# The mLSTM's second half moved up beside the last RWKV units, and the token-shift tile in buffers of its own

## The chip, the cores and the metric

The kernel runs on one core of a Trainium2 chip. The metric is the device time of one launch in microseconds; lower is better. TensorE runs at one of two clock levels, 1.2 and 2.4 GHz; the profile gives the granted clock as a share of the higher one.

## The reference, cut to what matters

A model of one mixing block with two kinds of recurrence, and two attention layers, on 1024 tokens of width 1024, in float32:

```python
z = rmsnorm(x, norm1) @ w_in              # 26 units of 128 columns, and 8 gate columns
y_r = rwkv7_group(z[:, :RW_COLS], ...)    # token shift, then 8 heads of 64: S <- S*decay + ..., y = S r
y_m = mlstm_group(z[:, RW_COLS:], ...)    # conv on q and k, then 4 heads of the chunkwise mLSTM, gated by o
x = x + concat([y_r, y_m]) @ w_out
x = x + ffn(rmsnorm(x, norm2))            # 22 pairs of gate and value columns, with a causal conv
for l in range(2): x = x + attention_layer(x, l)
```

The mLSTM divides its output by a normalizer, takes an RMS norm over each head, and multiplies by a gate:

```python
h = num / jnp.maximum(jnp.abs(den), jnp.exp(-m_t))[..., None]
y = head_rmsnorm(h) * mh_norm_g * sigmoid(o)
```

## The kernel before

Every float32 product of the projections is made from a high and a low part: `mm3` issues three matmuls of 128x128 by 128x512, weight-high by input-high, weight-high by input-low, weight-low by input-high. One such matmul is called a product here; they are numbered from 0 in the order of the program, and there are 11,328. Weights are loaded (`wraw`) by SP's DMA queue and split by ScalarE (`whi`) and VectorE or GpSimd (`wlo`), in `wsplit`. A helper `few` does the eight gate columns in 32 smaller matmuls on weights of its own (`few_split`).

The input projection runs in units of 128 columns, each in two halves of 512 tokens. 14 units belong to RWKV (`RW`), 12 to the mLSTM (`ML`). `unit` evicts a half: an RWKV unit is scaled into a tile `rq`, shifted by a token and mixed (`stage`) and stored to `pT` in memory. `rq`, with one buffer, is also the tile of the convolution and of the `few` weights. The scale `BC` of a half comes from `first_scale`: an rsqrt by VectorE (`nry`), transposes on TensorE (`p<-c_ident,nry`, the broadcast), and a copy.

Beside the products run two recurrences in small matmuls. RWKV works in 8 units of 128 tokens (units 0 to 7). For a unit it prepares operands, inverts a triangular matrix for eight heads (`Z`, `X`, their diagonals `ZD`, `XD`, `Y`, `GD`), refines it (`AA`, `GT`, `TT`), runs two chunks (`RH`, `UV`, state `S`, output `P`), and then normalizes and gates the output (`out`: `YS`, `yva`, `yry`, transposes into PSUM tile `e`, `YQ`, and `sg,wug`, the gate, into `e` again). The mLSTM works in 8 blocks of 128 tokens (`ml_block`): transposes of `rv`, keys, scores `SD`, the state `C`, the numerator `NUM`, denominator `den`, `HN` with its norm (`mr...`), transposes of `HN`, and the store of the result to `yd`. Blocks 0 to 3 are the first half, 4 to 7 the second.

PSUM banks come from pools: `e` (pool `pse`) has one bank. The operands of RWKV stand on the right side of the memory in pools `rc`, `re`, `ro` and others; `re`, with one buffer, holds the first operands of a unit. `ml1` is the mLSTM's second half; `rest` first closes RWKV's whole room (`right.close()`) and then opens pools `mx` and `my` and two banks for it. Behind it comes, for each half of the tokens (`half1`), the out projection, which loads the results (`xo<-yd`) and splits them (`act<-xo`), and the FFN. The out projection of the first half runs early; that of the second begins at product 2448, and needs the whole second half of the mLSTM.

A scheduler sets the order of each engine; an engine runs its instructions in that order. `pace(groups, start, n)` gives it a rule: product `start + i*n` may not be issued ahead of group i (a group is a run of small matmuls without another engine's work between them):

```python
for groups, start, n in self.paces:
    for i, g in enumerate(groups):
        j = int(start + i * n)
        if g is not None and j < len(self.gm):
            self.tc.add_manual_dep(self.gm[j].ins, g.ins.name, dep, reason="order")
```

So a pace is a deadline of the group, not its earliest time. `g2` is product 960. RWKV's groups are paced from `g2 + NB0`, 1160, four products apart; the 40 groups of `ml1` (ten to a block) from `g2 + NC0`, 2002, twelve apart, so that the last comes before product 2470.

Of the kernel before, what the change touches and what calls it, by code (L numbers as in the profile page):

```python
# [25 lines left out]
NEG = -1.0e30  # L26
NW1 = 26
NW2 = 52
NA0, NA, NM0, NM, NB0, NB, NC0, NCC, SP0, SP1 = 60, 4, 30, 12, 200, 4, 1042, 12, 7, 11
NS0 = 60  # L30
NG = 6
PA = 56, 1, 48, 1
# [96 lines left out]
class Kern:  # L129
# [170 lines left out]
    def block1(self, yd):  # L300
        nc, ap, tc = self.nc, self.ap, self.tc
        gR, gK, gV, gL = (self.dram([128, n, T], "pT") for n in (4, 4, 4, 2))
        gQ, gW, gO = (self.dram([128, 4, T], "pT") for _ in range(3))
# [3 lines left out]
                 + [(gO, j) for j in range(4)])  # L307
        RW = [12, 13] + list(range(12))
        ML = list(range(14, 26))
        right = ExitStack()  # L310
        with self.pools(stg=2, bcp=1, a1=2, psl=1) as (stg, bcp, a1, psl):
            BC = self.t(bcp, [128, 2, 512], "BC")
            acts = [None, self.new_act(a1)]
# [8 lines left out]
            def unit(j, halves, w=None, ps=None):  # L322
                w = w or self.wsplit(ap["w_in"][j])
                g, i = where[j]
                for hf in halves:
                    acc = self.gemm(w, acts[hf], ps=ps)
                    if j < 14:

                        rq = self.t(stg, [128, 515], "rq", bufs=1)[:, 0:513]
                        if hf == 0:  # L330
                            nc.vector.memset(rq[:, 0:1], 0.0)
                        else:
                            nc.vector.tensor_copy(rq[:, 0:1], shalo[:, j:j + 1])
                        self.tt(rq[:, 1:513], acc, BC[:, hf])
                        st = self.t(stg, [128, 512], "stage")
                        self.act(st, rq[:, 1:513], scale=omu[:, j:j + 1])
                        self.stt(st, rq[:, 0:512], self.par("mu", j), st)
                        if hf == 0:
                            nc.vector.tensor_copy(shalo[:, j:j + 1], rq[:, 512:513])
                        nc.sync.dma_start(g[:, i, hf * 512:hf * 512 + 512], st)  # L340
                        continue
                    st = self.t(stg, [128, 512], "stage")
                    if g is gQ:

                        rq = self.t(stg, [128, 515], "rq", bufs=1)
                        if hf == 0:
                            nc.vector.memset(rq[:, 0:3], 0.0)
                        else:
                            nc.vector.tensor_copy(rq[:, 0:3], halo[:, i])
                        self.tt(rq[:, 3:515], acc, BC[:, hf])  # L350
                        if hf == 0:
                            nc.vector.tensor_copy(halo[:, i], rq[:, 512:515])
                        cv = self.t(stg, [128, 512], "cv", bufs=1)
                        self.act(cv, rq[:, 0:512], AF.Identity, bias=cwh[:, 16 + i:17 + i], scale=cwh[:, i:i + 1])
                        for n in range(1, 4):
                            self.stt(cv, rq[:, n:n + 512], cwh[:, 4 * n + i:4 * n + i + 1], cv)
                        self.act(st, cv, AF.Tanh)
                        self.stt(st, st, 1.0, cv, op0=ALU.add, op1=ALU.mult)
                    else:
                        self.tt(st, acc, BC[:, hf])  # L360
                    nc.sync.dma_start(g[:, i, hf * 512:hf * 512 + 512], st)

            with self.pools(a0=2) as a0:
                acts[0] = self.new_act(a0)
                with self.pools(x0=4, nrm=2) as (xp, sp):
                    with self.pools(psw=4) as psw:
                        w = [self.wsplit(ap["w_in"][j]) for j in RW[:2]]
                        st = self.first_load(xp, sp, 0, acts[0])
                        self.first_scale(sp, psl, st, BC, 0)
                        for i in range(2):  # L370
                            unit(RW[i], (0,), w[i], psw)
                        st = self.first_load(xp, sp, 1, acts[1])
                        for j in RW[2:4]:
                            unit(j, (0,), None, psw)
                    self.first_scale(sp, psl, st, BC, 1)
                for j in RW[4:NG]:
                    unit(j, (0,))
                ws = self.few_split(stg, "cv", stg, ap["w_g"], 8, "rq")
                for hf in range(2):
                    sg = self.t(stg, [8, 512], "stage")  # L380
                    self.few(stg, ("stage", 2), ws, 8, acts[hf], sg)
                    self.tt(sg, sg, BC[0:8, hf])
                    nc.sync.dma_start(gG[:, hf * 512:hf * 512 + 512], sg)
                with self.pools(side="right", mr=1) as mr:
                    G = self.ml_gates(self.mk, mr, psl, gG)
                    for j in RW[NG:]:
                        unit(j, (0,))
                names = dict(rc=1, re=1, ro=1, r2=2, r3=3, rx=1, psm=2, psc=1, pse=1)
                R = dict(zip(names, right.enter_context(self.pools(side="right", **names))))
                rw = self.rwkv(R, gR, gK, gV, gL, yd[0])  # L390
                g0 = len(self.gm)
                ga = [x for _ in range(4) for x in next(rw)]
                for j in ML:
                    unit(j, (0,))
# [13 lines left out]
                self.pace(gb, g2 + NB0, NB)  # L408
                self.pace(ga, g0 + NA0, NA)

        def ml1(mx, my, ps):
            gm = self.ml_blocks(range(4, 8), self.mk, mx, my, ps, G, gQ, gW, gO, yd[1])
            self.pace(gm, g2 + NC0, NCC)

        if self.stop == "mix":
            right.close()
            with self.pools(mx=1, my=2, psl=1) as (mx, my, psl):
                ml1(mx, my, psl)
            self.mks.close()
            for i in range(2):  # L420
                for hf in range(2):
                    nc.sync.dma_start(
                        self.dbg["yT"].rearrange("(g k p) t -> p g k t", p=128, k=4)[:, i, :, hf * 512:(hf + 1) * 512],
                        yd[i][hf])
            return
        self.rest(yd, right, ml1)


    @contextmanager
# [57 lines left out]
        self.flush()  # L487
        return acc

    def rest(self, yd, right, ml1):  # L490
        self.psn = None
        ap = self.ap
        xd = [[self.dram([128, 512], "xd") for _ in range(2)] for _ in range(8)]
        F = [None, None]
        with self.pools(acA=2) as self.acA:
            with self.pools(**self.ffn_pools(0)) as P:
                right.close()
                with self.pools(side="right", mx=1, my=2, psl=2) as (mx, my, psl):
                    ml1(mx, my, psl)
                self.mks.close()  # L500
                F[0] = self.half1(0, P, self.acA, yd, xd)
                for _ in range(8):
                    next(F[0])
                rs = ExitStack()
                self.acB = rs.enter_context(self.pools(side="right", acB=2))
                with self.pools(side="right", psn=2) as self.psn, self.pools(side="right", **self.ffn_pools(1)) as P1:
                    F[1] = self.half1(1, P1, self.acB, yd, xd)
                    next(F[1])
                    for a0 in F[0]:
                        pass  # L510
                    for a1 in F[1]:
                        pass
# [624 lines left out]
        nc.vector.memset(C, 0.0)  # L1137
        return dict(bmd=bmd, TK=TK, DEC=DEC, trik=trik, C=C)

    def ml_blocks(self, blocks, mc, mx, my, psm, G, gQ, gW, gO, yd):  # L1140
        with self.collect() as g:
            for tb in blocks:
                self.ml_block(tb, mc, mx, my, psm, G, gQ, gW, gO, yd)
        return g

    def ml_block(self, tb, mc, mx, my, psm, G, gQ, gW, gO, yd):
        nc = self.nc
        bmd, TK, DEC, trik = (G[n] for n in ("bmd", "TK", "DEC", "trik"))
        C = G["C"]
# [6 lines left out]
        nc.sync.dma_start(rv, gW[:, :, ts_])  # L1156
        V1 = self.t(my, [128, 4, 130], "V1")
        nc.vector.memset(V1[:, :, 128:129], 1.0)
        pv = self.t(psm, [128, 4, 128], "p")
        for h in range(4):  # L1160
            self.tr(pv[:, h], rv[:, h], self.ident)
        self.act(V1[:, :, 0:128], pv)
# [7 lines left out]
        self.tt(DT, DT, trik[:, None, :].to_broadcast([128, 4, 128]), ALU.add, eng=nc.gpsimd)  # L1170
        for h in range(4):
            self.act(DT[:, h], DT[:, h], AF.Exp, bias=TK[:, tb, 0, h:h + 1])
        pk = self.t(psm, [128, 2, 128], "p")
        for j in range(2):
            self.tr(pk[:, j], QK[:, 2 + j], self.ident)
        KW = self.t(mx, [128, 4, 64], "KW")
# [2 lines left out]
        SD = self.t(mx, [128, 4, 128], "SD")  # L1179
        for i in range(2):  # L1180
            pr = slice(i * 64, i * 64 + 64)
            pst = self.t(psm, [128, 2, 128], "p")
            for h2 in range(2):
                self.mm(pst[:, h2], QK[pr, 2 + h2], QK[pr, h2])
            self.stt(SD[:, i:4:2], pst, 0.125, DT[:, i:4:2], op0=ALU.mult, op1=ALU.mult)
        NUM = self.t(mx, [128, 4, 130], "NUM")
        for i in range(2):
            pr = slice(i * 64, i * 64 + 64)
            pq = self.t(psm, [128, 2, 130], "p")
            for h2 in range(2):  # L1190
                self.mm(pq[:, h2, 0:129], QK[pr, h2], C[pr, h2, 0:129])
            for h2 in range(2):
                h = h2 * 2 + i
                self.act(NUM[:, h, 0:129], pq[:, h2, 0:129], scale=TK[:, tb, 3, h:h + 1])
        Cn = self.t(mc, [128, 2, 130], "C", bufs=2)
        pcs = self.t(psm, [128, 2, 130], "p")
        for h in range(4):
            h2, i = h // 2, h % 2
            self.mm(pcs[i * 64:i * 64 + 64, h2, 0:129], KW[:, h], V1[:, h, 0:129])
# [2 lines left out]
            pr = slice(i * 64, i * 64 + 64)  # L1202
            self.stt(Cn[pr, h2, 0:129], C[pr, h2, 0:129], DEC[pr, h, tb:tb + 1], pcs[pr, h2, 0:129])
        for h2 in range(2):
            pn = self.t(psm, [128, 2, 130], "p")
            for i in range(2):
                self.mm(pn[:, i, 0:129], SD[:, h2 * 2 + i], V1[:, h2 * 2 + i, 0:129])
            self.tt(NUM[:, 2 * h2:2 * h2 + 2, 0:129], NUM[:, 2 * h2:2 * h2 + 2, 0:129], pn[:, :, 0:129], ALU.add)
# [12 lines left out]
        self.ts(va, va, 1.0 / 128, 1e-6)  # L1221
        rs = self.rsqrt(mx, va, "mr")
        self.tt(HN, HN, rs[:, :, None].to_broadcast([128, 4, 128]))
        ph = self.t(psm, [128, 4, 128], "p")
        for h in range(4):
            self.tr(ph[:, h], HN[:, h], self.ident)
        YO = self.t(mx, [128, 4, 128], "SD")
# [489 lines left out]
```

## Time and profile before

| | |
|---|---|
| median of 3 runs | 3503.1 µs |
| runs | 3508.12, 3502.71, 3503.10 µs |
| the profiled execution's own time | 3496.53 µs |
| its span | 3494.7 µs |
| mean granted clock of TensorE | 0.984 |

The profile shows one execution on the chip. Times are microseconds from the start of the span. PE is TensorE's matmuls, PEld its weight loads, DVE VectorE, ACT ScalarE, POOL GpSimd, SPq the DMA queue of SyncE. A row of the timeline has start, duration, engine, line of the kernel, operation, written tile and read tiles, and the number of like instructions in a row; square brackets hold the idle time of the engine before it and what ended it. Almost every matmul has line 186 and every transpose line 189, since helpers issue them: they are told apart by their tiles. Matmul ends are modelled, so durations of matmuls in a row overlap.

### The profile page before, as it was taken

Reading aid. Unit: us, or ns where it says so; the run is one execution under the profiler, and the core shown is the slowest. Engines: PE = TensorE matmul, PEld = TensorE weight load, DVE = VectorE, ACT = ScalarE, POOL = GpSimd, SP = SyncE. Lnnn points to the kernel's source line nnn. Section 1 sums busy time; section 2 is a strip of 40 time slices with the busy share of each in tenths; the row PEclk is TensorE's granted clock in tenths of the full one; section 3 lists DMA queues with packets and bytes.
Section 4 is the critical chain, followed back from the end, with each engine's and each line's share of the span. In section 5 each row is a group of like instructions: output and inputs, shape, how many; then the busy total and the mean of one; then the engine's idle time right before and its main releaser. Section 6 shows DMA issues by size and latency. Waiting matters only on the chain.

```text
span 3494.7 us, 51106 instructions
## 1 busy us (share of the span) xinstructions
PE 3379.8 (97%) x18820; PEld 2730.9 (78%) x18820; DVE 2038.6 (58%) x4223; ACT 1609.1 (46%) x3244; POOL 702.6 (20%) x601
## 2 busy tenths in 40 slices
PE   7999999999899999999999999999999999999998
PEld 6777777777677777778888878888878888888886
DVE  6767767765655745467666762234776567712235
ACT  4467677654433433345555652122355456621222
POOL 1222122222122222242111111111321111111111
PEclk9999899999999999999999999999999999999999
DMA  4433233123333323333212121113531121211124
GB/s 149 155 115 103 79 112 102 56 68 111 102 113 94 128 91 91 94 121 89 55 55 66 45 88 58 43 53 110 158 98 55 48 67 51 79 53 60 50 71 142
DMA packets 196986, 303.51 MB, mean 87 GB/s; under 512 B 22976, under 2 KB 65600, under 8 KB 196736
## 3 DMA queue, kind: packets, MB, share of 16 engines
q1 hardware_dynamic: 196736, 300.25, 28.1%
q8 instruction: 148, 2.42, 0.3%
q14 instruction: 102, 0.84, 0.1%
HBM read 244.41 MB, written 38.98 MB: 81 GB/s over the span
## 4 chain that ended last, share of the span: by engine, by line
PE 51%; DVE 2%; ACT 2%; issue 1%; DMA 0%; SPq 0%; POOL 0%; DVEq 0%; ACTq 0%; POOLq 0%
PE p L186 31%; PE acc L186 10%; PE o L186 3%; PE t L189 3%; PE S L186 3%; ACT whi L166 0%; DMA qw<-qf 0%; DVE qf L172 0%; PE d L186 0%; DVE wlo L172 0%; SPq L1374 0%; DVE yt L172 0%; DVE dd L1458 0%; ACT act L166 0%; ACT dd L168 0%
## 5 line engine op out<-in xcount | busy, mean ns | idle before, releaser
L186 PE MATMUL p<-act,whi 128*128 128x512 f32 x5824 | 1893.4, 402 | 31.0 <-ACT act L166 22.1
L186 PEld LDWEIGHTS p<-act,whi 128*128 128x128 f32 x5824 | 1086.3, 190 | 265.5 <-ACT act L166 23.8
L186 PE MATMUL p<-act,wlo 128*128 128x512 f32 x2912 | 1162.4, 401 | 2.1 <-DVE wlo L172 2.0
L172 POOL TENSOR_TENSOR wlo<-wraw,whi 128x512 fp32r<-128x512 f32 (+1 forms) x366 | 501.8, 1371 | 1959.4 <-ACT whi L166 1738.7
L166 ACT ACTIVATE whi<-wraw 128x512 fp32r<-128x512 f32 x732 | 424.1, 620 | 777.2 <-PE p L186 324.0
L186 PEld LDWEIGHTS p<-act,wlo 128*128 128x128 f32 x2912 | 552.8, 190 | 123.0 <-DVE wlo L172 6.8
L172 DVE TENSOR_TENSOR wlo<-wraw,whi 128x512 fp32r<-128x512 f32 x366 | 286.4, 784 | 264.7 <-ACT whi L166 262.4
L168 ACT ACTIVATE dd<-dd,nm 128x256 f32<-128x256 f32 (+7 forms) x256 | 171.1, 669 | 107.5 <-DVE nm L1458 105.4
L166 ACT ACTIVATE th<-p 128x512 f32<-128x512 f32 x96 | 56.4, 588 | 307.5 <-PE p L186 287.1
L166 ACT ACTIVATE ph<-t 128x384 fp32r<-128x384 f32 (+1 forms) x248 | 135.4, 557 | 123.0 <-PE t L189 118.3
L172 DVE TENSOR_TENSOR pl<-t,ph 128x384 fp32r<-128x384 f32 (+1 forms) x248 | 156.2, 636 | 50.3 <-ACT ph L166 47.4
L183 DVE SCALAR_TENSOR_TENSOR th<-th,acc 128x512 f32<-128x512 f32 x64 | 43.9, 687 | 223.7 <-ACT th L166 223.5
L177 POOL TENSOR_SCALAR rx<-rd 128x128 f32<-128x128 f32 x128 | 72.1, 572 | 478.0 <-PE t L189 235.5
L189 PE MATMUL t<-c_ident,dd 128*128 128x128 f32 x900 | 152.8, 275 | 1.0 <-DVE yt L172 0.7
L172 DVE TENSOR_TENSOR xs<-xs,d 128x512 f32<-128x512 f32 x132 | 88.7, 684 | 98.8 <-PE d L186 97.5
L186 PE MATMUL o<-ph,V 128*128 128x256 f32 (+1 forms) x532 | 132.6, 282 | 1.7 <-ACT ph L166 1.6
L186 PE MATMUL o<-pl,V 128*128 128x256 f32 (+1 forms) x532 | 130.3, 291 | 0.1
L1458 DVE CUSTOM_DVE_ANT_0 dd<-S,strip 128x512 f32<-128x512 f32 (+3 forms) x160 | 91.5, 586 | 52.8 <-PE t L189 29.8
L189 PEld LDWEIGHTS t<-c_ident,dd 128*128 128x128 f32 x900 | 107.7, 141 | 11.1 <-DVE yt L172 1.5
L186 PE MATMUL d<-gl,whi 128*128 128x512 f32 x264 | 107.2, 406 | 6.3 <-DVE gl L172 6.3
L186 PE MATMUL d<-gh,whi 128*128 128x512 f32 x264 | 105.1, 411 | 7.0 <-DVE xs L172 5.2
L186 PEld LDWEIGHTS o<-ph,V 128*128 128x128 f32 x532 | 98.7, 190 | 14.7 <-ACT ph L166 4.3
(407 smaller groups left out, 5066.3 us busy)
## 6 DMA issues: line engine op xcount, KB each, us to landing
wraw<-in_w_in SPq DMA_DIRECT2D x332, 256.0 KB, 2.8
wraw<-in_w_up SPq DMA_DIRECT2D x176, 256.0 KB, 2.6
wraw<-in_w_out SPq DMA_DIRECT2D x96, 256.0 KB, 2.8
wraw<-in_w_dn SPq DMA_DIRECT2D x88, 256.0 KB, 2.7
pT<-stage SPq DMA_DIRECT2D x52, 256.0 KB, 3.8
qw<-qf SPq DMA_DIRECT2D x160, 64.0 KB, 2.0
xd<-xs SPq DMA_DIRECT2D x32, 256.0 KB, 3.0
yd<-yt SPq DMA_DIRECT2D x32, 256.0 KB, 2.3
```

The source lines that it names most:

```text
L166: return self.nc.scalar.activation(out, in_, func, scale=scale, **kw)
L168: return self.nc.scalar.activation(out, in_, func, bias=bias, scale=scale, **kw)
L172: (eng or self.nc.vector).tensor_tensor(out, a, b, op=op)
L177: (eng or self.nc.vector).tensor_scalar(out, a, s1, None, op0=op0)
L183: return self.nc.vector.scalar_tensor_tensor(out, a, s, b, op0=op0, op1=op1, **kw)
L186: return self.pe(self.nc.tensor.matmul(out, lhsT, rhs, start=start, stop=stop, **kw))
L189: return self.pe(self.nc.tensor.transpose(out, in_, ident))
L1458: nc.vector.tensor_tensor_reduce(dd[:, o:o + w], sps[:, :w], strip[:, o:o + w], -1.0, init, ALU.add, ALU.min, nm)
```

## The change

The shift of the RWKV units gets a tile `sh` with two buffers; `rq` stays with the convolution and the `few` weights. Pool `re` is opened in a stack of its own, `elems`. `ml1` closes that one alone, opens `mx` and `my` in its room, takes RWKV's bank `e` for its PSUM tiles instead of two banks of its own, and closes RWKV's remaining room behind it. It is paced from `g2 + 760`, product 1720, instead of 2002: the last group is due before product 2188.

```diff
-NA0, NA, NM0, NM, NB0, NB, NC0, NCC, SP0, SP1 = 60, 4, 30, 12, 200, 4, 1042, 12, 7, 11
+NA0, NA, NM0, NM, NB0, NB, NC0, NCC, SP0, SP1 = 60, 4, 30, 12, 200, 4, 760, 12, 7, 11
...
-        right = ExitStack()
+        right, elems = ExitStack(), ExitStack()
...
-                        rq = self.t(stg, [128, 515], "rq", bufs=1)[:, 0:513]
+                        rq = self.t(stg, [128, 513], "sh", bufs=2)
...
-                names = dict(rc=1, re=1, ro=1, r2=2, r3=3, rx=1, psm=2, psc=1, pse=1)
+                names = dict(rc=1, ro=1, r2=2, r3=3, rx=1, psm=2, psc=1, pse=1)
                 R = dict(zip(names, right.enter_context(self.pools(side="right", **names))))
+
+                R["re"] = elems.enter_context(self.pools(side="right", re=1))
...
-        def ml1(mx, my, ps):
-            gm = self.ml_blocks(range(4, 8), self.mk, mx, my, ps, G, gQ, gW, gO, yd[1])
+        def ml1():
+            elems.close()
+            with self.pools(side="right", mx=1, my=2) as (mx, my):
+                gm = self.ml_blocks(range(4, 8), self.mk, mx, my, R["pse"], G, gQ, gW, gO, yd[1], "e")
+            right.close()
             self.pace(gm, g2 + NC0, NCC)
...
-                right.close()
-                with self.pools(side="right", mx=1, my=2, psl=2) as (mx, my, psl):
-                    ml1(mx, my, psl)
+                ml1()
                 self.mks.close()
...
-    def ml_block(self, tb, mc, mx, my, psm, G, gQ, gW, gO, yd):
+    def ml_block(self, tb, mc, mx, my, psm, G, gQ, gW, gO, yd, tag):
...
-        pv = self.t(psm, [128, 4, 128], "p")
+        pv = self.t(psm, [128, 4, 128], tag)
```

Every PSUM tile of `ml_block` takes `tag` in this way.

The first place is TensorE at the sixth RWKV unit (`p_515`), the broadcast of the second half's scale (`p_454`), and the `few` products (`p_554` and `p_577`, 16 for each half of the tokens), as a piece of the difference of the two orders.

```order
 L186 MATMUL p_515<-act_115,whi_505 128x512
 L186 MATMUL p_515<-act_114,wlo_506 128x512
-L189 MATMUL p_454<-c_ident_60,nry_441 128x128 x4
 L186 MATMUL p_554<-act_114,rq_550 40x512
 L186 MATMUL p_554<-act_115,rq_550 40x512
```

```order
 L186 MATMUL p_577<-act_103,rq_550 40x512
 L186 MATMUL p_577<-act_104,rq_550 40x512
+L189 MATMUL p_454<-c_ident_60,nry_441 128x128 x4
 L186 MATMUL p_737<-act_114,whi_727 128x512
 L186 MATMUL p_737<-act_115,whi_727 128x512
```

The broadcast moved from ahead of the 32 `few` products to behind them.

On VectorE the low part of the `few` weights (`rq_550`) moved too; this is the place among the first loads (`act_115` are parts of the input) where it stands now.

```order
 L183 SCALAR_TENSOR_TENSOR act_115<-x_165,pk_58,act_114 128x512
 L172 TENSOR_TENSOR nacc_48_149<-nacc_48_149,nsq_54_169 128x512
+L172 TENSOR_TENSOR rq_550<-cv_548,rq_550 128x8x8
 L177 TENSOR_SCALAR gb_619<-gbx_617 128x2
 L183 SCALAR_TENSOR_TENSOR act_115<-x_172,pk_58,act_114 128x512
```

Before it stood behind the sixth shift.

The second place is TensorE in RWKV's last unit (7), at its chunks: first before, `p_9342` and `p_9384` being products of the FFN or out projection, `p_9432` of the FFN.

```order
L186 MATMUL P_7692<-RH_7701,TT_7640 64x64 x8
L186 MATMUL p_9342<-act_8682,wlo_9333 128x512
L186 MATMUL p_9342<-act_8682,whi_9332 128x512
L186 MATMUL p_9342<-act_8683,whi_9332 128x512
L186 MATMUL p_9342<-act_8682,wlo_9333 128x512
L186 MATMUL P_7692<-UV_7352,BT_7360 64x64 x8
L186 MATMUL p_9384<-act_8683,whi_9374 128x512
L186 MATMUL p_9384<-act_8682,wlo_9375 128x512
```

And the same place after:

```order
L186 MATMUL P_7692<-RH_7701,TT_7640 64x64 x8
L186 MATMUL P_7692<-UV_7352,BT_7360 64x64 x8
L186 MATMUL P_7692<-S_7720,AR_7139 64x64 x8
L186 MATMUL P_7692<-RH_7731,TT_7640 64x64 x8
L186 MATMUL P_7692<-UV_7352,BT_7360 64x64 x8
```

The products are gone from between them. It is so for all 302 small matmuls of this unit from product 1730 on; before, 168 products (1730 to 1898) lie among them.

The third place is TensorE at the first group of the mLSTM's second half (`rv` and `QK`): before, where unit 7's output (`e_7810`, `e_7821`) stands far above, with products all round.

```order
L186 MATMUL p_9594<-act_8682,whi_9584 128x512
L186 MATMUL p_9594<-act_8683,whi_9584 128x512
L186 MATMUL p_9594<-act_8682,wlo_9585 128x512
L189 MATMUL p_7898<-c_ident_60,rv_7894 128x128 x4
L189 MATMUL p_7918<-c_ident_60,QK_7892 128x128 x2
```

After:

```order
L186 MATMUL P_7692<-UV_7352,AM_7302 64x64 x16
L189 MATMUL e_7810<-c_ident_60,YS_7785 128x128 x4
L186 MATMUL e_7821<-sg_7070,wug_1126 128x128 x4
L189 MATMUL e_7887<-c_ident_60,rv_7883 128x128 x4
L186 MATMUL d_9226<-gl_9154,whi_9200 128x512
L186 MATMUL d_9226<-gh_9153,wlo_9201 128x512
L189 MATMUL e_7907<-c_ident_60,QK_7881 128x128 x2
```

The group came up to directly behind unit 7's output, and product 1730 stands behind it. The last transposes of `HN` stand at product 2226 after, at 2448 before; the out projection of the second half begins at 2442 after. From product 2472 on the orders agree.

## Rows read from the trace of the kernel before

**Rows 1.** The page: busy time of each engine, share of the span, instructions.

```profile
PE 3379.8 (97%) x18820; PEld 2730.9 (78%) x18820; DVE 2038.6 (58%) x4223; ACT 1609.1 (46%) x3244; POOL 702.6 (20%) x601
```

**Rows 2.** Windows: length, busy and count of each engine, clock, DMA share, GB/s.

```profile
50.00:60.00 10.00, 3.51 (x10) 1.79 (x11) 5.12 (x15) 1.92 (x3) 0.18 (x1) 0.60 0.40 131
...
731.50:789.60 58.10, 55.07 (x474) 42.02 (x472) 31.38 (x60) 30.49 (x56) 14.86 (x12) 1.00 0.23 69
...
951.60:985.00 33.40, 23.61 (x77) 16.63 (x77) 10.61 (x16) 9.76 (x19) 4.03 (x3) 0.80 0.43 126
985.00:1000.00 15.00, 15.00 (x66) 12.06 (x65) 8.01 (x9) 4.76 (x9) 3.95 (x3) 1.00 0.52 166
```

**Rows 3.** Timeline of TensorE at the `few` products.

```profile
52.02 1.04 PE L189 MATMUL p<-c_ident,nry 128*128 128x128 f32 x4 [4.24 <-DVE shalo L339]
57.53 9.78 PE L186 MATMUL p<-act,rq 128*40 128x512 f32 x32 [4.47 <-DVE rq L172]
```

**Rows 4.** Timeline of VectorE there: the last step of `nry`, the `few` weights.

```profile
51.71 0.15 DVE L183 SCALAR_TENSOR_TENSOR nry<-nrq,nry 128x4 f32<-128x4 f32 x1
...
57.25 0.22 DVE L172 TENSOR_TENSOR rq<-cv,rq 128x64 fp32r<-128x64 f32 x1 [0.54 <-ACT rq L166]
```

**Rows 5.** Timeline of TensorE in RWKV's last unit, its small matmuls.

```profile
731.96 0.41 PE L186 MATMUL m<-Y,GD 128*128 128x64 f16 x8
...
744.33 1.15 PE L186 MATMUL m<-AA,GT 64*64 64x64 f32 x32
...
756.15 1.14 PE L186 MATMUL P<-RH,TT 64*64 64x64 f32 x16
...
766.43 0.69 PE L186 MATMUL P<-UV,BT 128*64 128x64 f32 x16
...
768.80 1.15 PE L186 MATMUL P<-UV,AM 128*64 128x64 f32 x32
...
782.36 0.66 PE L189 MATMUL e<-c_ident,YS 128*128 128x128 f32 x4 [0.20 <-POOL YS L172]
```

**Rows 6.** Groups of 731–792 µs: busy, mean ns, then idle before and releaser.

```profile
L172 POOL TENSOR_TENSOR YQ<-YQ,BON 128x512 f32<-128x512 f32 x2 | 2.6, 1290 | 3.3 <-ACT YQ L168 3.3
L166 ACT ACTIVATE XD<-X 64x512 f16<-64x512 f16 x4 | 2.5, 629 | 0.1
...
L172 POOL TENSOR_TENSOR YS<-YS,yry 128x512 f32<-128x512 f32 x2 | 2.1, 1045 | 8.5 <-PE p L186 4.9 <-DVE yry L183 3.6
...
L166 ACT ACTIVATE UV<-P 64x512 f32<-64x512 f32 x2 | 1.2, 592 | 7.6 <-PE P L186 7.6
...
L172 DVE TENSOR_TENSOR S<-S,P 128x256 f32<-128x256 f32 x2 | 0.8, 417 | 4.0 <-PE P L186 4.0
...
L1028 DVE TENSOR_REDUCE yva<-YQ 128x8 f32<-128x512 f32 x1 | 0.7, 677 | 0.0
...
L183 DVE SCALAR_TENSOR_TENSOR yrq<-yrq,yva 128x8 f32<-128x8 f32 x3 | 0.5, 166 | 0.1
```

**Rows 7.** Timeline of TensorE in an earlier unit, at 386.6–407.1 µs, at half clock.

```profile
391.71 1.96 PE L186 MATMUL P<-RH,TT 64*64 64x64 f32 x16
```

**Rows 8.** Timeline of TensorE at the end of the mLSTM's second half.

```profile
938.01 0.61 PE L186 MATMUL p<-V,SD 128*128 128x129 f32 x4
...
950.99 0.63 PE L189 MATMUL p<-c_ident,HN 128*128 128x128 f32 x4 [0.42 <-DVE HN L172]
958.01 1.65 PE L186 MATMUL p<-act,whi 128*128 128x512 f32 x3 [6.39 <-ACT act L166]
...
963.30 0.92 PE L186 MATMUL p<-act,whi 128*128 128x512 f32 x3
```

**Rows 9.** Timeline of VectorE there, the last step of the block's norm.

```profile
950.15 0.69 DVE L172 TENSOR_TENSOR HN<-HN,mry 128x512 f32<-128x512 f32 x1
```

**Rows 10.** Timelines of SP's DMA queue and of ScalarE there: the first split.

```profile
958.71 10.41 SPq L539 DMA_DIRECT2D xo<-yd  x6
...
957.33 1.15 ACT L166 ACTIVATE act<-xo 128x512 fp32r<-128x512 f32 x2 [4.53 <-DMA yd<-SD]
```

More of the change, by code (lines that the diff above doesn't have):

```diff
@@ L409, in block1 @@
                 self.pace(ga, g0 + NA0, NA)
-        def ml1(mx, my, ps):
-            gm = self.ml_blocks(range(4, 8), self.mk, mx, my, ps, G, gQ, gW, gO, yd[1])
+        def ml1():
[3 more added lines that the diff above has]
+            right.close()
             self.pace(gm, g2 + NC0, NCC)
         if self.stop == "mix":
-            right.close()
-            with self.pools(mx=1, my=2, psl=1) as (mx, my, psl):
-                ml1(mx, my, psl)
-            self.mks.close()
+            ml1()
             for i in range(2):
@@ L425, in block1 @@
             return
-        self.rest(yd, right, ml1)
+        self.rest(yd, ml1)
     @contextmanager
@@ L488, in gemm, with rest @@
         return acc
-    def rest(self, yd, right, ml1):
+    def rest(self, yd, ml1):
         self.psn = None
@@ L496, in rest @@
             with self.pools(**self.ffn_pools(0)) as P:
-                right.close()
-                with self.pools(side="right", mx=1, my=2, psl=2) as (mx, my, psl):
-                    ml1(mx, my, psl)
+                ml1()
                 self.mks.close()
@@ L1138, in ml_gates, with ml_blocks @@
         return dict(bmd=bmd, TK=TK, DEC=DEC, trik=trik, C=C)
-    def ml_blocks(self, blocks, mc, mx, my, psm, G, gQ, gW, gO, yd):
+    def ml_blocks(self, blocks, mc, mx, my, psm, G, gQ, gW, gO, yd, tag="p"):
         with self.collect() as g:
             for tb in blocks:
-                self.ml_block(tb, mc, mx, my, psm, G, gQ, gW, gO, yd)
+                self.ml_block(tb, mc, mx, my, psm, G, gQ, gW, gO, yd, tag)
         return g
-    def ml_block(self, tb, mc, mx, my, psm, G, gQ, gW, gO, yd):
+    def ml_block(self, tb, mc, mx, my, psm, G, gQ, gW, gO, yd, tag):
         nc = self.nc
@@ L1172, in ml_block @@
             self.act(DT[:, h], DT[:, h], AF.Exp, bias=TK[:, tb, 0, h:h + 1])
-        pk = self.t(psm, [128, 2, 128], "p")
+        pk = self.t(psm, [128, 2, 128], tag)
         for j in range(2):
@@ L1181, in ml_block @@
             pr = slice(i * 64, i * 64 + 64)
-            pst = self.t(psm, [128, 2, 128], "p")
+            pst = self.t(psm, [128, 2, 128], tag)
             for h2 in range(2):
@@ L1188, in ml_block @@
             pr = slice(i * 64, i * 64 + 64)
-            pq = self.t(psm, [128, 2, 130], "p")
+            pq = self.t(psm, [128, 2, 130], tag)
             for h2 in range(2):
@@ L1195, in ml_block @@
         Cn = self.t(mc, [128, 2, 130], "C", bufs=2)
-        pcs = self.t(psm, [128, 2, 130], "p")
+        pcs = self.t(psm, [128, 2, 130], tag)
         for h in range(4):
@@ L1204, in ml_block @@
         for h2 in range(2):
-            pn = self.t(psm, [128, 2, 130], "p")
+            pn = self.t(psm, [128, 2, 130], tag)
             for i in range(2):
@@ L1223, in ml_block @@
         self.tt(HN, HN, rs[:, :, None].to_broadcast([128, 4, 128]))
-        ph = self.t(psm, [128, 4, 128], "p")
+        ph = self.t(psm, [128, 4, 128], tag)
         for h in range(4):
```

## The prediction

> **What bounds the kernel now.** I read the page's busy shares first: TensorE is busy 97% of the span [rows 1], so time is only to be won where it waits or runs at its lower clock, and lost where something opens a hole in its row of products. Next the windows [rows 2], a line for each stretch that the change touches. At 985–1000 µs 66 products fill 15.00 µs at clock 1.00: 0.2273 µs for a product, which prices all products below. At 50–60 and 951.6–985 the engine is far from full (3.51 of 10.00, 23.61 of 33.40) and its clock is 0.60 and 0.80: these two are the holes of before. At 731.5–789.6, the last RWKV unit, it is busy 55.07 of 58.10 at clock 1.00: no hole. That stretch is full only because products stand between the small matmuls.
>
> **Part 1, the shift tile.** The `few` weights and the shift shared one buffer, so the weights could be written only when the sixth shift was done: the low part at 57.25 [rows 4], and the 32 `few` products wait for it 4.47 µs, behind a wait of 4.24 µs for the last shift ahead of the broadcast [rows 3]. Afterwards the weights are split during the first loads and the products stand directly behind the sixth unit, ahead of the broadcast (both in the order shown above). They read nothing that is late then: `nry`, for the broadcast, is finished at 51.86 [rows 4], and 32 products from 47.6 on last till 54.9. So both waits go, 8.7; the 32 products took 9.78 µs [rows 3] where 32 × 0.2273 = 7.3 would do, since the idling had lowered the clock: 2.5 more. I take 10 of these 11.2, for the broadcast's own matmuls may wait for a bank. **−10** (−6 if the shift's evictions hold a bank for about 5 µs, −11).
>
> **Part 2, the end of mLSTM's second half.** It is the last thing that the second out projection waits for. Before, its last block is stored and read again at once (`xo<-yd`, 958.71), the split of the first tile waits 4.53 µs for the load, and the products begin at 958.01 after 6.39 µs, with further waits for each pair of tiles [rows 8, 10]. The whole stretch takes 33.40 µs for 77 products [rows 2], which is 77 × 0.2273 = 17.5 at full clock: 15.9 lost. After the change the last transposes stand at product 2226, over 200 products ahead of the projection (2442), and in the queues the loads and splits precede it. Weights that come late still cost a little: **−15** (−13 to −16).
>
> **Part 3, the last RWKV unit without cover.** Here the change costs. One PSUM bank, `e`, serves the units' output and now mLSTM's second half. Its first group thus stands behind unit 7's last use of that bank; and as the pace forbids product 1720 to be issued ahead of that group, all products stop till unit 7 is through. The order shows it: between `RH,TT` and `UV,BT` stood products, now none; the 168 products 1730–1898, that before lay among these matmuls, come behind them. So TensorE runs the chain alone, with its latency in the open. The chain, from rows [rows 5, 6]:
> - two levels of the inversion: each takes ScalarE Y 0.60, X about 0.6, two XD at 0.63, two ZD at 0.63, 3.7 in all, and two matmul groups at 0.41: 2 × 4.5 = 9.0;
> - the refinement: `AA,GT` twice at 1.15, three groups at 0.41 (3.5 on TensorE), and some seven evictions of 0.6 to 0.7, of which about 4.4 lie open: 7.9;
> - the two chunks of P: `RH,TT` 1.14, `UV,BT` 0.69, `S,AR` about 0.69, twice, and `UV,AM` 1.15: 6.2; evictions RH 0.68, UV 0.59 twice, S 0.42 twice, YS about 0.6: 3.3. Together 9.5;
> - the unit's output: mean 0.68 and 0.17, GpSimd 1.04, square 0.63, reduction 0.68, eleven small operations of 0.16 at a step of about 0.2 (2.2), GpSimd 1.05, transposes 0.66, four YQ at a step of about 0.38 (1.5), GpSimd 1.29, VectorE 0.69: 10.6. Before, GpSimd's 1.05 and its waits lay behind products;
> - mLSTM's transposes 0.63, and 1.0 for some twenty hand-overs.
>
> The sum is 38.6. TensorE's own 13.8 of it (the groups of the chain, twenty of them) are at full clock; but an engine so idle did not keep it: at 391.71 `RH,TT` took 1.96 instead of 1.14 [rows 7], a factor of 1.72, up to +9.9. I take 8, as the first groups still find the clock full. Then comes the return: at 958.01–963.30, behind an idle gap, 12 products took 5.29 µs where 2.73 would do [rows 8]: 2.5. The 168 products follow in the open, 168 × 0.2273 = 38.2. After: 38.6 + 8 + 2.5 + 38.2 = 87.3; before: 58.1 [rows 2]. **+29** (lower bound 37.6 + 38.2 − 58.1 = +18, without hand-overs and with the clock kept; upper +33, with 9.9 and double hand-overs).
>
> The Trainium skill ("TensorE: Matmul & The Clock Gate", Part 1, on HAM oscillation) puts the penalty of a throttled stretch at half of it: matmuls at half speed throughout would add 13.8 instead of 8, and make this term about 35. The row of 1.96 says less, and goes into the sum. The same page (Part 2, what each phase is for) says that matmuls stay in program order and only weight loads are pulled ahead; no row here shows a matmul overtaken or not, and by the page the products behind this chain cannot fill it; if they could, part 3 would come to nothing and the sum to −11.
>
> **Part 4, mLSTM's own tails.** Each of the four blocks ends in a chain without matmuls: NUM, den, HN, square, reduction, rsqrt, HN, and then transposes. In the last block of before it lasted from the end of the last `V,SD` at 938.62 to 950.99, 12.4 µs [rows 8], with VectorE shared: its rsqrt crawls between other operations, and HN, from 950.15, takes 0.69 [rows 9]. Alone it would be 0.41 + 0.51 + 0.69 + 0.63 + 0.68 + 0.16 + 2.2 + 0.69, about 6.3 with its hand-overs. Products that stand in the order between `V1,SD` and `HN`: 54, 66, 66 and 42 before, that is 9.5 µs or more each; 34, 16, 12 and 50 after: 7.7, 3.6, 2.7 and 11.4 µs. The deadline squeezes them: a product every 12 is held until its group. At 9.0, about midway (VectorE has less to do when products stall), the open rests are 1.3 + 5.4 + 6.3 + 0 = 13, and a little for the clock: **+14**. At 6.3 they are 2.7 + 3.6 = +6; at 12.4, 4.7 + 8.8 + 9.7 + 1.0 = +24.
>
> What costs nothing: mLSTM's loads come earlier; the idle chain of part 3, in which no product takes a weight, hides the first of them, and elsewhere a load that delays a weight costs about 1.7 µs (10.41 for six tiles [rows 10]); the single bank, in the middle of a block, has 12 products (2.7 µs) from group to group over an eviction of 0.4 to 0.7 [rows 6]; if that cover failed, a block would lose about 1 µs a group, and this is in the upper bound of part 4. From product 2472 on the order is the same as before.
>
> **Sum.** −10 − 15 + 29 + 14 = +18. The profiled execution took 3496.5 (span 3494.7): about 3514.5 by its measure. The runs of before have a median of 3503.1, 6.6 above it: I predict **3521** beside that median. This kernel's runs can't tell under 0.2%, 7 µs, from no change (they lie between 3502.7 and 3508.1).
>
> **Rivals.**
> - *No difference.* Chain at full clock (+18) and mLSTM's tails unloaded (+6), against gains of 25: −1, about 3502. For it: ScalarE and VectorE are free during the chain. Against it: `RH,TT` at 1.96 [rows 7], in a stretch less empty than this will be.
> - *The other side: faster.* The chain is worked in two halves of the heads, and if one half's evictions hide behind the other's matmuls, its length comes near to TensorE's 13.8 plus the output's 10.6, about 25: the part costs 25 + 38.2 − 58.1 = +5, with tails of +6 the sum is −14: 3489. It decides once the chain is below 31. Against it: between 731.96 and 744.33 [rows 5] products were at hand for each gap and the two levels still took 12.4, the 744.33 to 756.15 of the refinement 11.8, so the latency is not small.
> - *The gain at 951 fails.* If the loads of the second half still come late (behind weights in SP's queue, 10.41 µs for six tiles [rows 10]), part 2 is 0: +33, 3536. Against it: the loads stand far ahead in the queue.
>
> **Chances.** The forecast, with sizes within their bounds, 0.72; the gain at 951 missing 0.08; no difference 0.13; faster 0.07. So faster 0.07, same 0.13, slower 0.80. The range leaves out the fastest case and part of the second, and on top what goes beyond +35: 3503 to 3538; without the other cases it would be 3511 to 3535.
>
> **What would show it.** Right: `few` products from about 48 without a wait; from about 721 a stretch of some 45 µs with no product, TensorE mostly idle, clock about half; `p/e<-c_ident,HN` waits for VectorE in the second and third block; no wait for `act` before the second out projection. Wrong: products among the `P` matmuls in the trace; the chain under 31 µs; the out projection still waiting for `xo`.

## The result and the profile after

The changed kernel takes 3539.85 µs, the median of 6 runs (3538.03 to 3550.25), against 3502.93 of before (3499.78 to 3508.12): a ratio of 1.0111, with an interval of 1.0096 to 1.0127. It is slower, as forecast, but by 37 µs where 18 were predicted; the time lies just outside the range, which ended at 3538.

The first place went as predicted. The timeline of TensorE after shows the `few` products directly behind the sixth unit, at full clock, 7.58 µs instead of 9.78 [rows 3], and the broadcast behind them without a wait:

```profile
47.60 7.58 PE L186 MATMUL p<-act,rq 128*40 128x512 f32 x32
55.02 0.60 PE L189 MATMUL p<-c_ident,nry 128*128 128x128 f32 x4
56.13 0.74 PE L186 MATMUL p<-act,whi 128*128 128x512 f32 x2 [0.51 <-DVE stage L172]
```

Then RWKV's last unit, the same view: product 1728 starts at 733.70, product 1730 at 780.72, and what lies between is small matmuls with gaps, of which these are a few.

```profile
742.41 1.97 PE L186 MATMUL m<-AA,GT 64*64 64x64 f32 x32 [0.21 <-ACT AA L166]
...
752.37 1.96 PE L186 MATMUL P<-RH,TT 64*64 64x64 f32 x16 [0.78 <-DVE TT L172]
755.01 1.12 PE L186 MATMUL P<-UV,BT 128*64 128x64 f32 x16 [0.68 <-ACT UV L166]
...
764.51 1.97 PE L186 MATMUL P<-UV,AM 128*64 128x64 f32 x32
774.33 1.12 PE L189 MATMUL e<-c_ident,YS 128*128 128x128 f32 x4 [7.85 <-POOL YS L172]
777.04 2.08 PE L186 MATMUL e<-sg,wug 128*128 128x128 f32 x8 [1.60 <-ACT YQ L168]
779.96 1.12 PE L189 MATMUL e<-c_ident,rv 128*128 128x128 f32 x4 [0.84 <-DVE YQ L172]
780.72 0.78 PE L186 MATMUL d<-gl,whi 128*128 128x512 f32 x1
```

Each of these groups takes about 1.7 times as long as in [rows 5]: `AA,GT` 1.97 for 1.15, `RH,TT` 1.96 for 1.14. The longest gap, 7.85, is the norm of the unit's output, on ScalarE, VectorE and GpSimd. The first mLSTM group is released by the eviction of bank `e` (`YQ`). The windows after, columns as in [rows 2], show the open stretch, the 168 products behind it, the mLSTM's second half, and the begin of the second out projection:

```profile
733.70:780.70 47.00, 24.44 (x311) 20.63 (x310) 12.99 (x33) 16.62 (x31) 4.63 (x4) 0.59 0.02 7
780.70:833.60 52.90, 50.67 (x227) 37.35 (x226) 28.82 (x61) 24.39 (x44) 12.38 (x9) 0.98 0.39 118
833.60:1007.80 174.20, 151.05 (x651) 115.86 (x650) 99.89 (x193) 66.59 (x127) 33.35 (x25) 0.94 0.31 93
1007.80:1023.50 15.70, 14.30 (x61) 11.23 (x61) 4.66 (x8) 3.89 (x7) 2.57 (x2) 1.00 0.33 101
```

In the first line TensorE is busy 24.44 of 47.00 at clock 0.59, where before, with the 168 products among its matmuls, it was 55.07 of 58.10 at 1.00. The last line has 61 products and nearly no gap: the hole of 951.6–985 [rows 2, 8] is gone.

To see where time goes or comes from when orders are nearly alike, I take the starts of the products numbered at these stages and their differences, in µs, from two traces of each kernel (the second of before and of after are experiments f4 and g2):

| products | before | before again | after | after again | mean change | predicted |
|---|---|---|---|---|---|---|
| 0–200 | 70.7 | 70.7 | 60.4 | 60.5 | −10.2 | −10 |
| 200–300 | 24.5 | 24.6 | 25.3 | 29.1 | +2.7 | 0 |
| 300–1300 | 432.8 | 446.7 | 442.5 | 438.2 | +0.6 | 0 |
| 1300–1728 | 193.7 | 193.8 | 196.6 | 198.3 | +3.7 | 0 |
| 1728–1898 | 58.6 | 58.6 | 99.9 | 100.1 | +41.4 | +29 |
| 1898–2440 | 157.3 | 157.4 | 174.3 | 175.2 | +17.4 | +14 |
| 2440–2500 | 32.4 | 31.1 | 15.7 | 15.7 | −16.1 | −15 |
| 2500–11300 | 2493.1 | 2494.7 | 2490.6 | 2493.8 | −1.7 | 0 |

The changes add up to +37.8, like the medians.

### The profile page after: what moved, and what is told of

Read it like the earlier page. It is cut to its first block, busy times and chain, and to the rows that moved or that the text cites. A ratio compares the mean times of both kernels' runs of the same rounds, so it can differ in the third digit from the quotient of the medians.

```text
span 3536.3 us, 51107 instructions
## 1 busy us (share of the span) xinstructions
PE 3395.9 (96%) x18820; PEld 2743.8 (78%) x18820; DVE 2044.9 (58%) x4223; ACT 1610.7 (46%) x3244; POOL 706.7 (20%) x601
## 4 chain that ended last, share of the span: by engine, by line
PE 51%; DVE 2%; ACT 2%; issue 1%; DMA 0%; SPq 0%; POOL 0%; DVEq 0%; ACTq 0%; POOLq 0%
PE p L186 31%; PE acc L186 10%; PE o L186 3%; PE t L189 3%; PE S L186 3%; ACT whi L166 0%; DVE qf L172 0%; DMA qw<-qf 0%; PE d L186 0%; DVE wlo L172 0%; DVE dd L1458 0%; DVE yt L172 0%; SPq L1374 0%; ACT dd L168 0%; ACT ph L166 0%
## 5 line engine op out<-in xcount | busy, mean ns | idle before, releaser
L172 DVE TENSOR_TENSOR pl<-t,ph 128x384 fp32r<-128x384 f32 (+1 forms) x248 | 156.3, 637 | 50.2 <-ACT ph L166 47.2
L1458 DVE CUSTOM_DVE_ANT_0 dd<-S,strip 128x512 f32<-128x512 f32 (+3 forms) x160 | 91.6, 586 | 52.9 <-PE t L189 29.8
```

What stands on the lines that cost most here:

```text
L172: (eng or self.nc.vector).tensor_tensor(out, a, b, op=op)
L1458: nc.vector.tensor_tensor_reduce(dd[:, o:o + w], sps[:, :w], strip[:, o:o + w], -1.0, init, ALU.add, ALU.min, nm)
```

## The experiments

Times are medians; before's median lay between 3501.0 and 3502.8 beside them.

**e1: the shift tile alone.**

```diff
-                        rq = self.t(stg, [128, 515], "rq", bufs=1)[:, 0:513]
+                        rq = self.t(stg, [128, 513], "sh", bufs=2)
```

> The kernel before with the shift tile in its own buffers alone. In the profile of the changed kernel product 200 came 10.7 us earlier than before, but product 1300 only 0.1 us earlier, with the same order of matmuls and nearly the same waits between, at a lower mean clock. Theory A (this early gain is really lost again, because the RWKV units of that stretch set their own pace): 0 us against before, 3500 to 3506, and the lead of product 200 gone by product 1300. Rival B (the clock fell more often in that one execution by chance): about 10 us faster, 3490 to 3496, and the lead still there at product 1300.

3479.4 (3473.63 to 3483.63), a ratio of 0.9935 (0.9922 to 0.9947): 22 faster, more than either theory had. Products 0–200 take 60.3, as in the changed kernel; but 300–1300 take 426.6, at a higher mean clock. The order of its matmuls differs from that of before at several places between products 263 and 1048; whether that is why the clock fell less, no run shows. Theory A, that the gain is lost again, falls. The windows of products 300–1300, of this kernel first:

```profile
94.60:521.20 426.60, 403.75 (x3528) 313.60 (x3527) 299.44 (x660) 284.71 (x585) 95.57 (x70) 0.98 0.38 116
```

and of the kernel before as first profiled:

```profile
104.50:537.30 432.80, 411.39 (x3528) 320.31 (x3527) 295.75 (x662) 283.73 (x585) 95.09 (x70) 0.96 0.37 113
```

**e2: the changed kernel, paced from g2 + 940.**

```diff
-NA0, NA, NM0, NM, NB0, NB, NC0, NCC, SP0, SP1 = 60, 4, 30, 12, 200, 4, 760, 12, 7, 11
+NA0, NA, NM0, NM, NB0, NB, NC0, NCC, SP0, SP1 = 60, 4, 30, 12, 200, 4, 940, 12, 7, 11
```

> The changed kernel, but the second half of the mLSTM is paced from g2 + 940 (product 1900) instead of g2 + 760. In its order products stand among all matmuls of the last RWKV unit, as before the change. Theory A (the deadline ahead of the unit's end is what stops the products): the stretch without products is gone, -41; tails with 32, 28, 18 and 39 products for cover cost about 10; the gain of 16 at the second out projection stays: 3490 to 3502. Rival B (the shared bank and room cost the time themselves, wherever the deadline stands): still slower than before, 3515 to 3540.

3516.84 (3513.68 to 3517.9), ratio 1.0042 (1.003 to 1.0054). Between products 1728 and 1730 lie 0.6 µs: the open stretch is gone, as theory A had it. But 1898–2440 take 190.3, where 157.3 were taken before with about as many small matmuls (168 and 164): what I had given 10 costs 33. So theory A is right on the stretch, and the time is the one that rival B had. The waits of TensorE of this kernel in that stage, 793.3–983.6 µs (in total, times, longest), begin thus:

```profile
PE e L189 <- DVE HN L172: 9.3, 4, 4.6
PE p L186 <- DVE cv L172: 6.1, 3, 5.5
PE e L186 <- ACT NUM L166: 2.7, 2, 1.7
```

**e3: the same pace as changed, two other banks.**

```diff
-                gm = self.ml_blocks(range(4, 8), self.mk, mx, my, R["pse"], G, gQ, gW, gO, yd[1], "e")
+                gm = self.ml_blocks(range(4, 8), self.mk, mx, my, R["psm"], G, gQ, gW, gO, yd[1], "m")
```

> The changed kernel with the pace as changed, from g2 + 760, but the mLSTM's second half takes the two PSUM banks of RWKV's pool psm (tag m, last used when the triangular matrix is inverted) instead of the one bank e (last used by the unit's output). In its order 188 small matmuls stand without a product, instead of 268, and the tails have 39, 40, 63 and 66 products. Theory A (the bank sets how far the first group must wait for the unit): only the inversion and refinement lie open, about +12, tails +1, the projection's gain of 16 stays: 3490 to 3506. Rival B (the room of re is what the group waits for): no change against the changed kernel, about 3540.

3493.13 (3483.61 to 3501.08), ratio 0.9978 (0.9967 to 0.9989): theory A. This one edit is worth 47 µs. Products 1728–1730 lie 18.8 apart instead of 47.0, and 1898–2440 take 144.4. Its timeline of TensorE shows the first group (`rv`) already behind the refinement, and products at once behind it:

```profile
747.88 1.97 PE L186 MATMUL m<-AA,GT 64*64 64x64 f32 x32
751.43 0.23 PE L186 MATMUL m<-X,ZD 128*128 128x64 bf16 x1 [1.58 <-DVE ZD L172]
751.64 1.09 PE L189 MATMUL m<-c_ident,rv 128*128 128x128 f32 x4
752.52 0.58 PE L186 MATMUL m<-X,ZD 128*128 128x64 bf16 x7
752.91 0.78 PE L186 MATMUL d<-gl,whi 128*128 128x512 f32 x1
```

**e4: these two banks, paced from g2 + 900.** The edit of e3, and 900 for 760.

> As the run with the banks of psm, but paced from g2 + 900, where the deadline binds nothing: the first group stands at product 1792 of its own accord, the last transposes at 2219, and products stand among all matmuls of the last RWKV unit. Tails have 27, 65, 61 and 71 products. Theory A: no open stretch, tails +3, the projection's gain of 16 kept, early gain between 0 and 10: 3476 to 3492, faster than before. Rival B (the mLSTM's work beside the last unit itself slows it, by ScalarE and VectorE): 3500 or more.

3477.5 (3467.84 to 3481.59), ratio 0.9929 (0.9915 to 0.9943): faster than both kernels, theory A. Its trace is of the fastest run, 3467.84. No open stretch (0.6), 1898–2440 in 141.2, 2440–2500 in 15.7. In its stretch 722–960 the waits for `HN` are down to one:

```profile
PE m L189 <- DVE HN L172: 0.7, 1, 0.7
```

**f1: the kernel before, paced from g2 + 760.** The line of the table of numbers alone, 1042 to 760.

> The kernel before with its pace alone moved to g2 + 760: the mLSTM's second half keeps two PSUM banks and a room of its own, which open only when RWKV's whole room is closed; no shift tile of its own. Its order has 270 small matmuls without a product at 1730, like the changed kernel's 268, and tails with 46, 33, 38 and 66 products instead of 34, 16, 12 and 50. Theory A (a deadline ahead of the last unit's end opens that unit, whatever the bank): the stretch costs +41 to +46 between products 1728 and 1898 as in the changed kernel, tails little, the projection's gain of 16 stays: 3524 to 3536. Rival B (the shared bank and room are what costs): 3500 or less.

3530.73 (3527.98 to 3538.41), ratio 1.0089 (1.0074 to 1.0105): theory A. The open stretch is there (49.4 from product 1728 to 1730), with two banks and a room of its own. But 1898–2440 take 153.7, with no wait for `HN` among the larger ones, which the waits of TensorE at 733–1000 µs begin with:

```profile
PE e L189 <- POOL YS L172: 7.8, 1, 7.8
PE p L189 <- DMA rv<-pT: 3.2, 1, 3.2
PE e L186 <- ACT YQ L168: 2.7, 2, 1.6
PE p L186 <- DVE cv L172: 2.5, 1, 2.5
```

I read the second row as the room: opened only when RWKV's is closed, it gets its loads late. No run tests this.

**f2: the changed kernel without the shift tile's buffers.** The edit of e1, undone in the changed kernel.

> The changed kernel without the shift tile's own buffers (rq as before). Theory A (the early gain is mostly lost again by product 1300 in this order, by a clock that falls for longer): about as the changed kernel, 3536 to 3544. Rival B (the early gain of 10 stays to the end, and the changed kernel would be 10 slower without it): 3547 to 3554.

3561.33 (3559.89 to 3566.38): 21 slower than with the tile, twice what even rival B had; theory A falls again. Products 0–200 take 73.1 (−12.7 with the tile), 300–1300 446.2.

**f3: the changed kernel with the old pace, g2 + 1042.**

> The changed kernel with the old pace, from g2 + 1042: the room and the single bank e alone. No stretch without products; the tails have 54, 22, 22 and 30 products, and the last transposes stand at 2472, in the second out projection's way. Theory A (one bank makes the four blocks longer, so that their tails lie open even with a late deadline): +10 to +20 against before, 3512 to 3522. Rival B (only the early pace costs): 3490 to 3503.

3508.26 (3506.14 to 3514.36), ratio 1.0025 (1.0011 to 1.0038). It lies between the two ranges, 3.7 under theory A's and 5.3 above rival B's. But e1, with the tile alone, took 3479.4, so room and bank cost 29 here: 1898–2440 take 162.6, and 2440–2500 31.7, the hole of before, since the last transposes stand at 2472.

**f4: the kernel before once more.**

> The kernel before once more, unchanged, for a second profile of it. It is to show how much the lower clock between products 300 and 1300 differs between executions of one order. Theory A (it differs by a few us and the changed order has more of it): product 1300 at 535 to 539, with 30 to 36 us at the lower clock up to there. Rival B (the kernel before was merely lucky in the profile shown): product 1300 at 541 or later.

3511.24, one run. Rival B: product 1300 starts at 551.5 instead of 537.3, with the same order and no other stage differing by more than 1.6. The window of its products 300–1300, to be held against 432.80 at 0.96 above:

```profile
104.80:551.50 446.70, 418.99 (x3527) 325.40 (x3526) 298.42 (x662) 283.89 (x584) 94.43 (x70) 0.94 0.37 110
```

TensorE's idle time rose by 6.3 (27.7 for 21.4) and its busy time by 7.6 at a lower clock. The other three kernels without the tile took 446.2, 445.9 and 452.0 (f2, f1, g1). So the first profile of before is the shortest of five there.

**g1: the fastest version without the tile.** The tile's edit undone in e4.

> The version with the banks of psm and the late pace (the fastest so far, 3477.5), without the shift tile's own buffers. Taking the tile out of the changed kernel cost 21, though its trace shows a lead of only 10.7 at product 200. Theory A (the wait and the few products at the lower clock are the whole of it, about 11, and the rest was chance): 3486 to 3491. Rival B (the tile is worth about 20, the order of the RWKV stretch that comes with it included): 3495 to 3501, with product 1300 some 20 us later than in the version with the tile.

3498.32 (3489.93 to 3502.52): rival B. The tile is worth 21 again. Of its trace, 13.1 lie in products 0–200 and 15.1 in 300–1300.

**g2: the changed kernel once more.**

> The changed kernel once more, unchanged, for a second profile. Theory A (the clock between products 300 and 1300 differs by several us between executions, and the stretch without products does not): between products 1728 and 1730 again 46 to 48 us, between 1898 and 2440 within 3 us of the first profile's 174, and the lead at product 1300 anywhere from +3 to -7 against the profile of before. Rival B (the open stretch itself differs as much): 1728 to 1730 more than 2 us away.

3543.43, one run. Theory A: 46.3 for 47.0, 175.2 for 174.3. In two executions of this order the open stretch cost the same. 300–1300 took 438.2 for 442.5.

**h1: the changed kernel, groups 15 products apart.** 15 for 12 in the table of numbers.

> The changed kernel with its groups 15 products apart instead of 12 (first deadline as changed, last at product 2305). In its order the tails of the four blocks have 29, 38, 41 and 55 products instead of 34, 16, 12 and 50; bank e is kept. Theory A (the second and third tail lie open because the deadlines leave them 16 and 12 products): the waits for HN fall from 9.4 to under 4 and the stretch from product 1898 to 2440 from 174 to about 162 to 168; 3528 to 3535. Rival B (one bank makes the blocks' steps serial, whatever the spacing): the stretch stays within 3 us of 174, 3537 to 3543.

3533.65 (3528.68 to 3541.19), ratio 1.0088 (1.007 to 1.0106): inside theory A's range, but its interval overlaps that of the changed kernel (1.0096 to 1.0127), so the 6 µs between the medians are not sure. The trace sides with theory A: 1898–2440 take 167.3, and the waits for `HN` fall to 4.9, where under 4 was expected:

```profile
PE e L189 <- POOL YS L172: 7.8, 1, 7.8
PE e L189 <- DVE HN L172: 4.9, 3, 1.9
```

## Why the prediction was right in kind and wrong in size

**Part 1 (−10)** was right at its place: −10.2. Its worth to the end is larger, 21 to 22 by three pairs of kernels (e1 and before, f2 and after, g1 and e4). The place itself gives 10 to 13 of it. The rest lies mostly in products 300–1300, where the kernels with the tile ran at a higher clock (0.98 in e1, 0.95 and 0.96 in the two traces of after, 0.96 in e4; without the tile 0.96 and 0.94 before, 0.94 in f2 and g1). But that stage differs by 14 between two executions of one order (f4), and the orders of each pair differ there too, so why the rest is there is open.

**Part 2 (−15)** was right: −16.1, and the projection no longer waits for the loads and splits. (The row that it read as a wait for the load names the store `yd<-SD` [rows 10]; the sum does not hang on it.) f3 shows the counterpart: when the last transposes stay at 2472, the gain is not there.

**Part 3 (+29): the mechanism and its size were right.** The chain was put at 38.6, and 8 for its clock: 46.6. It measures 47.0 and 46.3. So close a fit is partly luck: TensorE was busy 24.44 where 13.8 + 8 = 21.8 were priced, for an earlier unit's output (`YS` at 734.42) stood in the stretch too, and idle 22.56 where 24.8 were. At full clock its matmuls would have cost 16.9, an estimate (55.07 busy before, less 168 × 0.2273); they took 24.44, so the clock cost 7.5. The Trainium skill's reading ("TensorE: Matmul & The Clock Gate", Part 1, on HAM oscillation: half of the throttled time) had given 13.8. The trace gives less: the clock stood at its lower level for 38.5 of the 47.0 µs (0.59 on the mean), and the groups took 1.7 times as long there, not twice. The row decides for the smaller. The stage measures +41.4 because 56 small matmuls of the mLSTM, which stood behind product 1898 before, lie in it now. A small matmul costs 0.17 there before (157.3 less 6.4 idle and 541 × 0.2273, over 164), so an estimated 9.5 moved from the next stage: this one is +32, at its upper bound (recorded as +33; its own terms add up to 32.1). The 3 too many lie in the 168 products behind the chain: they took 52.9, where 38.2 + 2.5 + 9.5 = 50.2.

That a deadline ahead of the unit's end opens it, not the room, f1 shows (the pace alone: 49.4) and e2 (a late pace in the new room: 0.6). How far it opens, the bank decides (e3: 18.8).

**Part 4 (+14) is the step that failed in size.** With the 9.5 counted back the tails cost 17.4 + 9.5 = 27, above the bound of 24. (Without any such counting, parts 3 and 4 together measure 41.4 + 17.4 = 58.8, where 43 were forecast.) The waits that I priced were not the reason: they come in the second and third block, as forecast, and the open rests were to be 13, while the waits for `HN` are 9.4. These are the waits of TensorE after, at 733.7–1008 µs:

```profile
PE e L189 <- DVE HN L172: 9.4, 3, 4.9
PE e L189 <- POOL YS L172: 7.9, 1, 7.9
PE p L186 <- DVE cv L172: 7.1, 2, 6.1
PE p L186 <- ACT a L166: 3.6, 3, 1.7
```

Two things were missing. First, waits of the FFN (`cv`, `a`), 10.7 in all, 0.4 before. The longest, 6.12, is read from the two timelines of the same kernel, TensorE and ScalarE:

```profile
963.25 0.79 PE L186 MATMUL p<-gh,whi 128*128 128x512 f32 x1 [6.12 <-DVE cv L172]
```

```profile
956.40 0.63 ACT L166 ACTIVATE act<-xo 128x512 fp32r<-128x512 f32 x1 [2.06 <-DMA xo<-yd]
956.94 0.61 ACT L166 ACTIVATE whi<-wraw 128x512 fp32r<-128x512 f32 x1
957.46 0.61 ACT L166 ACTIVATE act<-xo 128x512 fp32r<-128x512 f32 x1
957.98 0.80 ACT L168 ACTIVATE cv<-a,pk 128x512 f32<-128x512 f32 x1
...
961.25 0.63 ACT L166 ACTIVATE act<-xo 128x512 fp32r<-128x512 f32 x1 [1.95 <-DMA xo<-yd]
961.78 0.61 ACT L166 ACTIVATE cv<-cv 128x512 f32<-128x512 f32 x1
```

The splits that part 2 rejoiced to find early stand ahead of two steps of the FFN's convolution on ScalarE, and wait there for their loads. That is not the whole of it: in e4 a split stands ahead of the same step with a longer wait,

```profile
892.12 0.63 ACT L166 ACTIVATE act<-xo 128x512 fp32r<-128x512 f32 x1 [3.21 <-DMA xo<-yd]
892.65 0.62 ACT L166 ACTIVATE cv<-cv 128x512 f32<-128x512 f32 x1
```

and TensorE still waits little for the FFN:

```profile
PE p L186 <- ACT a L166: 1.1, 2, 0.8
PE p L186 <- DVE cv L172: 0.8, 1, 0.8
```

In e3 these waits are 2.4, in f1 2.8, with two banks as in e4; in e2 and h1, with one bank as after, 7.6 and 4.3. So among the kernels with early splits they are larger with the one bank; by what path, no run shows. Second, the clock. This is the stage before, columns as in [rows 2]:

```profile
789.60:946.90 157.30, 150.89 (x709) 117.17 (x708) 99.37 (x206) 73.35 (x140) 35.61 (x27) 0.99 0.36 108
```

After, TensorE is busy 151.05 in 174.20 at 0.94, with 56 small matmuls fewer. That is 9.7 of lower clock (151.05 less 150.89 − 9.5), where I had put "a little", about 1. With 16.8 more idle time it makes the 27.

What stands behind both is the one bank, and in part the deadlines 12 products apart. Since the small matmuls of the stages differ from kernel to kernel, I compare products 1728–2500, in which each kernel has the same 472 of them: before 248.4, after 289.8; with 15 products instead of 12, 282.0 (h1); with two banks and the same pace 271.4 (f1) and 241.3 (e3). Even with late deadlines one bank takes 267.9 (e2) where two take 227.5 (e4). The banks of e3 differ from `e` in two ways, their number and their last user. In f1 the two banks open only behind RWKV, so it has the number without the earlier last user: 18 of the 48 between after and e3 go with the number and 30 with the last user, as far as single traces and f1's other room allow. How much of the 18 is serial evictions is not settled.

**What was left out of the sum.** Stages 200–300 and 1300–1728 took 2.7 and 3.7 more, and the prediction has no term for them. The first differs by 3.8 between the two executions of after. For the second the timeline shows one new wait of 2.35 for `YS` ahead of product 1728. It goes with the room: all kernels in which `re` is closed by itself have this wait, of 1.0 to 2.4, and take 195.1 to 199.3 there, whatever their tile, pace and bank; before, e1 and f1 lack it and take 193.7 to 194.1.

**The sum.** It was made against one execution of before. That execution was short in 300–1300; the medians and the mean of two traces agree on 37 to 38, so the miss of 19 is part 4 with 13, then 6.4 for the stages left out, and 3 of part 3, less small gains. The runs also give the sum by edits, in medians: the tile −22 and −21 (e1 against before, after against f2); the early pace alone +30 and +32 (f1 against before, after against f3); room and bank +29 and +31 (f3 against e1, f2 against f1). Each is worth about the same whichever of the others stands beside it. So room and bank cost as much as the early pace, and they do so at the old pace too. The whole move of the mLSTM costs 60 (f2 against before), where parts 2 to 4 gave it 28, and the tile gains 22 where part 1 had 10: that the sum was off by 19 only is luck, since these two misses partly cancel. What the edits give beyond the stages named in the sum lies for the most part outside products 0–200 and 1728–2500; where, single traces can't tell.

**The rivals.** "Faster" and "no difference" needed a chain below 31 or tails at 6: both measured otherwise. The gain at 951 did not fail.

## What to carry to other kernels

Look, in the order, for what a deadline waits for: a pace that demands a group ahead of the end of a long dependent chain stops the filler work until the chain is through, and the bank or room for which the group must wait decides how far. Here choosing other banks for the same moved work was worth 47 µs, and the early schedule with the single bank was worse than the late one that it was to replace. Price a stall with its lower clock, and look at which queues the early work now stands in front of; and take two traces of the kernel before, since one execution may be short by as much as a term of the sum: 14 µs here, where the terms were 10 to 29. Where a change has several parts, run each edit alone: a sum can come near while its parts do not.

## What the runs showed that I had not expected

One order, run twice, took 432.8 and 446.7 µs for the same thousand products, by 6.3 of idle time and by the clock (0.96 and 0.94), with all other stages within 1.6. And a 10 µs wait removed at the start was worth 21 at the end, three times over.
